# Eight tiles of the adaLN modulation move from the first phase to the fourth gate and the output projection

## The chip, the cores and the metric

The kernel runs on one core of a Trainium2 chip. The metric is device time in microseconds (us), the median of the runs shown; lower is better. Below, PE is the matrix engine (TensorE), DVE the vector engine, ACT the scalar engine, POOL GpSimd, and SP the engine that issues most DMAs.

## What is computed

One layer of a diffusion backbone over 256 latent tokens and 256 context tokens of width 2048, in float32:

```python
mod = silu(c) @ w_ada + b_ada                 # 6 x 2048 values: sh1, sc1, g1, sh2, sc2, g2
h  = rmsnorm(x) * (1 + sc1) + sh1             # hc likewise for the context
parts = split(h @ w_in)                       # ten projections of width 512
y  = sum_i sigmoid(h @ w_gate[i] + b_gate[i]) * (branch_i @ w_branch[i])   # 4 branches
x  = x + g1 * (y @ w_out)
h2 = rmsnorm(x) * (1 + sc2) + sh2
x  = x + g2 * ((silu(h2 @ w1) * (h2 @ w3)) @ w2)
```

The four branches are neighbourhood attention, a bidirectional gated DeltaNet, a Fourier mix and a spatial gating unit.

## The kernel before

Every weight streams through SBUF once. A weight tile is 1 MB (128 x 4 x 512 floats; in the first phase half of that). Each 1 MB tile is cut in two halves, and each half is split in two parts for accuracy: ACT casts it to `whi` (line 393), DVE subtracts to get `wlo` (line 395). PE then multiplies a half with 12 matmuls of 512 columns (hi x hi, lo x hi, hi x lo, for 2 k-tiles and 2 token tiles; lines 423 and 443), so a 1 MB tile is worth 24 matmuls.

The modulation needs 96 tiles of `w_ada`, 1 MB each, numbered t = 0 to 95. Two of them go over PE. Tiles below 32 (sh1, sc1) are multiplied twice on DVE, for latent and context (lines 358, 364). Each of the tiles 32 to 95 is one DVE instruction over 128 x 2048 floats with a sum (line 370), and a short read of the accumulator. These are the "later modulation": 32 to 47 are g1, 48 to 79 are sh2 and sc2 (needed when the second norm starts, `a2_lane`, line 1571), 80 to 95 are g2 (needed at the end).

The stages in order of time, with PE as the engine that all feed: the first phase (four projections of latent and context, in eight groups of two k-tiles, with the modulation tiles 0 to 31), the projections 7, 5, 6, 4, the gates 3, 2 and 0 with their branches (projection 8 inside gate 3), projection 9, the fourth gate (`gate_branch(1, ...)`, the DeltaNet's), the output projection, then w1/w3 and w2 of the feed-forward.

A list `plan` (lines 245 to 285) holds every load in one order, and SP issues the loads in it. `w_ada` tiles and all weight tiles after the first phase share one pool of three 1 MB buffers, `raw` (line 177; the half-size weight tiles of the first phase have two buffers of their own). A load is issued when a buffer is released: by the DVE multiplication for a `w_ada` tile, by the second `wlo` for a weight tile. `whi` and `wlo` have three buffers each (lines 178, 179), so a split runs at most two halves ahead of the half that PE reads. `queue` (line 248) spreads `n_ada` modulation tiles evenly behind the weight tiles of a stage:

```python
def queue(srcs, n_ada=0):
    for j, src in enumerate(srcs):
        plan.append(("w", src, 4))
        for _ in range(n_ada * (j + 1) // len(srcs) - n_ada * j // len(srcs)):
            if ada_rest:
                plan.append(("ada", ada_rest.pop(0), 4))
```

The first `ATAIL` of the later tiles stand in the first phase instead, two behind each of the four weight tiles of its last group (lines 246, 255, 262 to 267).

The order of instructions on each engine is fixed when the program is built. A small planner (`Issue`, line 61) keeps a model of the engines' clocks and takes steps of "lanes" (generators) as they come ready; `ada_lane` (line 330) gives a later tile to DVE when at least two halves stand ready for PE or when it has waited `slack` (0.5 us) after its modelled arrival (lines 366 to 371). On the chip each engine then works strictly through its own list.

Of the kernel before, what the change touches and what calls it, by code (L numbers as in the profile page):

```python
# [36 lines left out]
NMATS = 512  # L37

AHEAD = 3000
CFG = {'cvpos': 3, 'cv': 0, 'qv': 0, 'dn': 0, 'ev': 2000, 'evp': 0, 'evx': 0, 'evf': 0, 'evA': 0, 'ahead': 3000, 'adahp': 0, 'proj': {7: 2, 4: 2, 5: 2, 6: 2, 8: 2, 9: 2}, 'gate': {2: 1, 3: 1, 0: 1, 1: 3}, 'wout': [4, 4, 4, 0], 'hopp': 0.2, 'hopb': 0.25, 'hop': 0.2, 'win': 0.5, 'eps': 0.1, 'nz': 1, 'ndn': 11, 'nout': 4, 'groups': [[0, 2], [2, 2], [4, 2], [6, 2], [8, 2], [10, 2], [12, 2], [14, 2]], 'pe': [1, 18], 'pa': 5, 'atail': 8, 'nproj': 2, 'ngate': [9, 0, 8], 'start': 'a0 s0 x0 x1 s1 a16 w0 a1 a17 x2 w1 x3 w2 w3 s2 s3 s4', 'px1': 2, 'psp': 3, 'hoppA': 0.25, 'winA': 0.5, 'winA0': 1, 'hopA': 0.1, 'cw': [0, 0], 'ph1': 1, 'pseed': 0, 'pevac': 1, 'slack': 0.5}  # L40

GROUPS = tuple(tuple(g) for g in CFG.get('groups', ((0, 2), (2, 2), (4, 4), (8, 4), (12, 4))))


ATAIL = CFG['atail']
PE_ADA = tuple(CFG.get('pe',(0, 1, 2, 4, 5, 6, 7, 8, 10, 12, 14)))

# [6 lines left out]
class Event:  # L54


    def __init__(self):
        self.t = None


class Issue:
# [8 lines left out]
    def __init__(self):  # L70
        self.tune(CFG.get("hopA", CFG["hop"]), CFG.get("winA", CFG["win"]), CFG.get("hoppA", CFG["hopp"]), CFG.get("winA0", 3.0))
        self.now = 0.0
# [21 lines left out]
    def _turn(self, lane):  # L94
# [18 lines left out]
        else:  # L113
            window = self.win0 if lane[0] < 4 else self.win
            ready = lane[3] + ((self.HOP if lane[0] < 4 else CFG["hopb"]) if lane[5] not in (None, what) else 0.0)
            if ready > self.now + CFG["eps"] or self.clk[what] > self.now + window:
                return False
# [1731 lines left out]
```

## Time and profile before

| | us |
|---|---|
| median of 3 runs | 1753.32 (1749.28 to 1759.31) |
| the profiled execution's own time | 1752.79 |
| its span, first to last instruction | 1751.0 |
| PE busy / DVE busy / ACT busy in the span | 1702.5 / 1213.6 / 950.5 |
| later-modulation multiplications on DVE | 64, in 152.0 |
| mean granted TensorE clock | 0.998 |

Times in the rows are us from the start of the span. The ends of matmuls are modelled, so PE counts as busy through gaps shorter than a matmul; the count of matmuls in a stretch is the surer measure.

### The profile page before, as it was taken

The page shows a single profiled execution, that of the slowest core. Times are in us where ns is not written, and L with a number is a line of the kernel's source. Part 1 is how long each engine was busy: PE and PEld are TensorE (multiplying, and loading weights), DVE is VectorE, ACT ScalarE, POOL GpSimd, SP SyncE. Part 2 cuts the span into 40 slices and gives each one's busy share as a digit, 9 for nine tenths or more (in the row PEclk, how much of TensorE's full clock was granted, in tenths as well). Part 3 has the DMA queues.
Part 4 walks back from the last instruction along what each step waited for, and adds up shares of the span by engine and source line. Part 5 has one row for each costly group of instructions (what it writes and reads, how often), then busy time and mean ns, then how long its engine had stood idle before and what let it go on. Part 6 is the DMA issues. An engine that isn't in the chain of part 4 may idle for free.

```text
span 1751.0 us, 21765 instructions
## 1 busy us (share of the span) xinstructions
PE 1702.5 (97%) x8297; PEld 1395.0 (80%) x8297; DVE 1213.6 (69%) x1522; ACT 950.5 (54%) x1329; POOL 140.3 (8%) x136
## 2 busy tenths in 40 slices
PE   3999999999999999999999999999999999999998
PEld 2777887778788877988888878888888888888887
DVE  5999988885989865767776665555665555454554
ACT  5799977765556566235544474444444444433332
POOL 1000000210211153211101000000000000000000
PEclk9999999999999999999999999999999999999999
DMA  8677787656875655468777645666666655555553
GB/s 317 244 255 254 263 323 261 233 214 233 274 279 176 235 191 199 174 230 303 289 285 267 262 146 215 240 240 240 234 233 235 259 192 192 193 198 199 204 204 108
DMA packets 62461, 406.94 MB, mean 232 GB/s; under 512 B 7730, under 2 KB 8546, under 8 KB 16786
## 3 DMA queue, kind: packets, MB, share of 16 engines
q1 hardware_dynamic: 56164, 386.43, 60.4%
q0 software_dynamic: 4464, 16.49, 3.1%
q10 hardware_dynamic: 1728, 2.62, 0.4%
q8 instruction: 65, 1.06, 0.2%
q14 instruction: 40, 0.33, 0.0%
HBM read 401.29 MB, written 4.23 MB: 232 GB/s over the span
## 4 chain that ended last, share of the span: by engine, by line
PE 62%; issue 2%; POOL 1%; DMA 1%; ACT 0%; DVE 0%; POOLq 0%; ACTq 0%; DVEq 0%
PE acc L423 57%; PE acc L443 2%; POOL l L1177 1%; DMA raw<-w_gate 1%; PE ps L1694 1%; PE ps L1269 0%; POOL mg L1386 0%; PE ps L1258 0%; PE ps L1308 0%; PE ps L1211 0%; PE ps L1218 0%; PE ps L1280 0%; PE ps L1286 0%; PE ps L1290 0%; PE ps L1550 0%
## 5 line engine op out<-in xcount | busy, mean ns | idle before, releaser
L395 DVE TENSOR_TENSOR wlo<-raw,whi 128x1024 fp32r<-128x1024 f32 x532 | 667.9, 1257 | 422.0 <-ACT whi L393 416.9
L393 ACT CAST whi<-raw 128x1024 fp32r<-128x1024 f32 x532 | 560.3, 1055 | 574.1 <-PE acc L423 509.7
L423 PE MATMUL acc<-whi,hL 128*128 128x512 f32 x704 | 230.5, 398 | 0.0
L423 PE MATMUL acc<-whi,hH 128*128 128x512 f32 x704 | 224.5, 400 | 1.5 <-ACT acc L1361 0.8
L423 PE MATMUL acc<-wlo,hH 128*128 128x512 f32 x704 | 218.3, 391 | 1.0 <-DVE wlo L395 0.8
L423 PE MATMUL acc<-whi,h2L 128*128 128x512 f32 x684 | 213.4, 391 | 0.0
L423 PE MATMUL acc<-whi,h2H 128*128 128x512 f32 x684 | 211.8, 391 | 0.0
L423 PE MATMUL acc<-wlo,h2H 128*128 128x512 f32 x684 | 210.7, 389 | 0.0
L370 DVE SCALAR_TENSOR_TENSOR raw<-raw,cb 128x2048 f32<-128x2048 f32 x64 | 152.0, 2375 | 17.3 <-DMA raw<-w_ada 17.0
L423 PEld LDWEIGHTS acc<-wlo,hH 128*128 128x128 f32 x704 | 131.8, 188 | 30.4 <-DVE wlo L395 3.5
L423 PEld LDWEIGHTS acc<-whi,hL 128*128 128x128 f32 x704 | 132.3, 188 | 28.0 <-issue 0.7
L423 PEld LDWEIGHTS acc<-whi,hH 128*128 128x128 f32 x704 | 128.3, 189 | 28.5 <-ACT whi L393 1.4
L423 PEld LDWEIGHTS acc<-wlo,h2H 128*128 128x128 f32 x684 | 128.4, 188 | 26.7
L423 PEld LDWEIGHTS acc<-whi,h2L 128*128 128x128 f32 x684 | 128.4, 188 | 26.6
L423 PEld LDWEIGHTS acc<-whi,h2H 128*128 128x128 f32 x684 | 127.6, 188 | 26.1
L423 PE MATMUL acc<-whi,uL 128*128 128x512 f32 x340 | 105.0, 389 | 0.0
L423 PE MATMUL acc<-whi,uH 128*128 128x512 f32 x340 | 104.8, 389 | 0.0
L423 PE MATMUL acc<-wlo,uH 128*128 128x512 f32 x340 | 104.6, 389 | 0.0
L358 DVE SCALAR_TENSOR_TENSOR junk<-raw,cb 128x2048 bf16<-128x2048 f32 x30 | 68.6, 2285 | 11.3 <-ACT cb L522 11.2
L423 PEld LDWEIGHTS acc<-whi,uL 128*128 128x128 f32 x340 | 63.8, 188 | 13.3
L423 PEld LDWEIGHTS acc<-wlo,uH 128*128 128x128 f32 x340 | 63.8, 188 | 13.2
L423 PEld LDWEIGHTS acc<-whi,uH 128*128 128x128 f32 x340 | 63.7, 188 | 13.1
(390 smaller groups left out, 2161.9 us busy)
## 6 DMA issues: line engine op xcount, KB each, us to landing
raw<-w SPq DMA_DIRECT2D x132, 1024.0 KB, 4.8
raw<-w_ada SPq DMA_DIRECT2D x96, 1024.0 KB, 5.4
raw<-w_gate SPq DMA_DIRECT2D x64, 1024.0 KB, 4.9
raw<-w_in SPq DMA_DIRECT2D x24, 1024.0 KB, 5.6
raw<-w_in SPq DMA_DIRECT2D x32, 512.0 KB, 5.3
raw<-w_branch SPq DMA_DIRECT2D x16, 1024.0 KB, 4.9
raw<-w_out SPq DMA_DIRECT2D x16, 1024.0 KB, 4.8
bg<-b_gate POOLq DMA_DIRECT2D x16, 256.0 KB, 4.0
```

The lines of the kernel that those rows point to most:

```text
L358: V.scalar_tensor_tensor(junk, raw, 1.0, cb, ALU.mult, ALU.mult, accum_out=modA[:, 0, t:t + 1])
L370: V.scalar_tensor_tensor(raw, raw, 1.0, cb, ALU.mult, ALU.mult, accum_out=mod[:, t:t + 1])
L393: S.copy(hi, raws[e][:, 2 * q:2 * q + 2])
L395: V.tensor_tensor(lo, raws[e][:, 2 * q:2 * q + 2], hi.bitcast(F32), ALU.subtract)
L423: PE.matmul(acc, xx[:, kt0 + j, off:off + P], ww[:, j], start=start and n == 0 and not seeded, stop=stop and n == 5, skip_group_check=seeded)
L443: PE.matmul(acc[:, cs], xx[:, kt0 + j, off:off + P], ww[:, j, cs], start=n0 + n + i == 0, stop=n0 + n == 7 and i == 5, skip_group_check=c > 0)
L1177: G.tensor_tensor(dst.rearrange("p h (b i) -> p h b i", b=4), src[:, u0:u0 + 4].unsqueeze(2).to_broadcast([P, 4, 4, 32]), mats[:, M_BD:M_B ...
L1694: PE.transpose(tp[:, P * h:P * h + P], us[tt][:, P * h:P * h + P], ident)
```

## The change

`ATAIL` (`atail`) goes from 8 to 0, the fourth gate's share of modulation tiles (`ndn`) from 11 to 15 and the output projection's (`nout`) from 4 to 8. All other settings and all code are the same.

```diff
-CFG = {... 'ndn': 11, 'nout': 4, ... 'atail': 8, 'nproj': 2, 'ngate': [9, 0, 8], ...}
+CFG = {... 'ndn': 15, 'nout': 8, ... 'atail': 0, 'nproj': 2, 'ngate': [9, 0, 8], ...}
```

The tiles are taken from one list in order, so the numbers move up: the eight behind the projections are now 32 to 39 (they were 40 to 47), gate 3 has 40 to 48, gate 0 has 49 to 56, projection 9 has 57, the fourth gate 58 to 72 (was 66 to 76), the output projection 73 to 80 (was 77 to 80), and the feed-forward 81 to 95 as before. The count of tiles changes in three stages only: eight fewer in the first phase, four more in the fourth gate, four more in the output projection.

## Rows read from the trace of the kernel before

**Rows 1.** The page: busy us, share and instructions of each engine.
```profile
PE 1702.5 (97%) x8297; PEld 1395.0 (80%) x8297; DVE 1213.6 (69%) x1522; ACT 950.5 (54%) x1329; POOL 140.3 (8%) x136
```
**Rows 2.** Windows by stage: PE, PEld, DVE, ACT, POOL busy (count), clock, DMA share, GB/s.
```profile
40.00:205.00 165.00, 160.65 (x763) 128.55 (x762) 161.59 (x202) 151.38 (x298) 0.00 (x0) 1.00 0.71 251
205.00:239.30 34.30, 34.30 (x159) 28.05 (x158) 30.28 (x33) 30.42 (x58) 0.00 (x0) 1.00 0.90 333
239.30:330.00 90.70, 86.51 (x405) 69.77 (x404) 77.29 (x109) 67.44 (x93) 9.44 (x13) 0.98 0.71 258
804.80:916.00 111.20, 111.20 (x507) 92.00 (x507) 84.51 (x77) 56.72 (x65) 11.70 (x8) 1.00 0.77 285
916.00:982.70 66.70, 66.70 (x300) 55.22 (x299) 49.38 (x51) 31.48 (x38) 4.53 (x2) 1.00 0.74 272
```
**Rows 3.** Windows of line 370 alone: DVE busy (instructions, accumulator reads included).
```profile
205.00:239.30 34.30, 18.37 (x16) 1.00 0.90 333
804.80:916.00 111.20, 24.06 (x20) 1.00 0.77 285
916.00:982.70 66.70, 11.48 (x10) 1.00 0.74 272
```
**Rows 4.** The chain that ended last, a piece of the feed-forward: start us, us, what.
```profile
1199.22 41.53 PE acc L423 x183
```
**Rows 5.** What PE waited for between 236 and 330: total, times, longest.
```profile
PE ps L933 <- DVE rc L928: 2.5, 1, 2.5
PE ps L888 <- DVE kna L884: 1.6, 1, 1.6
```
**Rows 6.** Timeline of ACT, then DVE, 260 to 264: start, us, instruction [idle before].
```profile
260.25 1.05 ACT L393 CAST whi<-raw 128x1024 fp32r<-128x1024 f32 x1 [2.94 <-DMA raw<-w_in]
262.61 0.31 ACT L750 ACTIVATE rn<-sqs,gpar 128x16 f32<-128x16 f32 x1
...
263.24 0.69 DVE L884 TENSOR_TENSOR kna<-kna,rn 128x512 f32<-128x512 f32 x1
```
**Rows 7.** Timeline of SP's issues in the fourth gate, 849 to 883.
```profile
849.79 0.33 SPq L324 DMA_DIRECT2D raw<-w_ada  x1
855.12 0.33 SPq L324 DMA_DIRECT2D raw<-w_gate  x1
860.04 0.33 SPq L324 DMA_DIRECT2D raw<-w_ada  x1
861.18 0.33 SPq L324 DMA_DIRECT2D raw<-w_gate  x1
867.25 0.33 SPq L324 DMA_DIRECT2D raw<-w_gate  x1
868.39 0.33 SPq L324 DMA_DIRECT2D raw<-w_ada  x1
873.68 0.33 SPq L324 DMA_DIRECT2D raw<-w_gate  x1
882.81 0.33 SPq L324 DMA_DIRECT2D raw<-w_gate  x1
```
**Rows 8.** Timeline of DVE, 834 to 879: splits and multiplications that release those buffers.
```profile
834.44 2.29 DVE L370 SCALAR_TENSOR_TENSOR raw<-raw,cb 128x2048 f32<-128x2048 f32 x1 [2.08 <-DMA raw<-w_ada]
853.86 1.23 DVE L395 TENSOR_TENSOR wlo<-raw,whi 128x1024 fp32r<-128x1024 f32 x1 [1.49 <-ACT whi L393]
859.93 0.08 DVE L370 DVE_READ_ACCUMULATOR raw<-raw,cb 128x1 f32 x1
867.14 0.08 DVE L370 DVE_READ_ACCUMULATOR raw<-raw,cb 128x1 f32 x1
869.83 3.82 DVE L395 TENSOR_TENSOR wlo<-raw,whi 128x1024 fp32r<-128x1024 f32 x2 [0.28 <-ACT whi L393]
877.52 0.08 DVE L370 DVE_READ_ACCUMULATOR raw<-raw,cb 128x1 f32 x1
877.52 1.22 DVE L395 TENSOR_TENSOR wlo<-raw,whi 128x1024 fp32r<-128x1024 f32 x1
```
**Rows 9.** Timeline of PE: the first matmuls on two of those halves.
```profile
858.47 0.62 PE L423 MATMUL acc<-whi,hH 128*128 128x512 f32 x2
872.07 0.62 PE L423 MATMUL acc<-whi,hH 128*128 128x512 f32 x2
```
**Rows 10.** Windows around the wait for `rc`: columns as in Rows 2.
```profile
309.00:312.50 3.50, 1.03 (x9) 0.76 (x7) 3.43 (x8) 0.59 (x1) 1.23 (x1) 1.00 0.76 269
312.50:316.50 4.00, 4.00 (x19) 3.59 (x18) 2.38 (x5) 2.02 (x3) 0.00 (x0) 0.57 0.67 236
316.50:320.00 3.50, 3.50 (x23) 3.05 (x22) 1.90 (x5) 1.65 (x4) 0.00 (x0) 1.00 0.37 154
```

More of the change, by code (lines that the diff above doesn't have):

```diff
@@ L39 @@
 AHEAD = 3000
-CFG = {'cvpos': 3, 'cv': 0, 'qv': 0, 'dn': 0, 'ev': 2000, 'evp': 0, 'evx': 0, 'evf': 0, 'evA': 0, 'ahead': 3000, 'adahp': 0, 'proj': {7: 2, 4: 2, 5: 2, 6: 2, 8: 2, 9: 2}, 'gate': {2: 1, 3: 1, 0: 1, 1: 3}, 'wout': [4, 4, 4, 0], 'hopp': 0.2, 'hopb': 0.25, 'hop': 0.2, 'win': 0.5, 'eps': 0.1, 'nz': 1, 'ndn': 11, 'nout': 4, 'groups': [[0, 2], [2, 2], [4, 2], [6, 2], [8, 2], [10, 2], [12, 2], [14, 2]], 'pe': [1, 18], 'pa': 5, 'atail': 8, 'nproj': 2, 'ngate': [9, 0, 8], 'start': 'a0 s0 x0 x1 s1 a16 w0 a1 a17 x2 w1 x3 w2 w3 s2 s3 s4', 'px1': 2, 'psp': 3, 'hoppA': 0.25, 'winA': 0.5, 'winA0': 1, 'hopA': 0.1, 'cw': [0, 0], 'ph1': 1, 'pseed': 0, 'pevac': 1, 'slack': 0.5}
+CFG = {'cvpos': 3, 'cv': 0, 'qv': 0, 'dn': 0, 'ev': 2000, 'evp': 0, 'evx': 0, 'evf': 0, 'evA': 0, 'ahead': 3000, 'adahp': 0, 'proj': {7: 2, 4: 2, 5: 2, 6: 2, 8: 2, 9: 2}, 'gate': {2: 1, 3: 1, 0: 1, 1: 3}, 'wout': [4, 4, 4, 0], 'hopp': 0.2, 'hopb': 0.25, 'hop': 0.2, 'win': 0.5, 'eps': 0.1, 'nz': 1, 'ndn': 15, 'nout': 8, 'groups': [[0, 2], [2, 2], [4, 2], [6, 2], [8, 2], [10, 2], [12, 2], [14, 2]], 'pe': [1, 18], 'pa': 5, 'atail': 0, 'nproj': 2, 'ngate': [9, 0, 8], 'start': 'a0 s0 x0 x1 s1 a16 w0 a1 a17 x2 w1 x3 w2 w3 s2 s3 s4', 'px1': 2, 'psp': 3, 'hoppA': 0.25, 'winA': 0.5, 'winA0': 1, 'hopA': 0.1, 'cw': [0, 0], 'ph1': 1, 'pseed': 0, 'pevac': 1, 'slack': 0.5}
 GROUPS = tuple(tuple(g) for g in CFG.get('groups', ((0, 2), (2, 2), (4, 4), (8, 4), (12, 4))))
```

## The prediction

> **What bounds the kernel now.** I read the page first, then the windows by stage, then who waited for whom, and last the timelines of SP, DVE and PE in the stages whose load the change alters. The page says PE: 97% busy, DVE 69%, ACT 54% [rows 1]. Since PE's busy time hides short gaps, I checked it against a clean price. In the feed-forward 183 matmuls of 512 columns take 41.53 us, 0.227 each [rows 4], so a 1 MB weight tile (24 matmuls) is worth 5.45 us of PE. The fourth gate has 20 such tiles, 109 us by that price, and takes 111.2 us, its transposes included; the output projection's first twelve take 65 of 66.7 [rows 2]. PE has no idle time in either. In the end of the first phase (205 to 239.3), where the eight tiles are multiplied now, PE is also fed throughout: 34.3 busy of 34.3 us [rows 2]. The part of the first phase where DVE is the tight engine (161.6 of 165 us busy, PE 160.7) lies before it, from 40 to 205. None of the eight tiles is there: the window from 205 to 239.3 holds 16 instructions of line 370, eight multiplications and eight accumulator reads [rows 3].
>
> So the change takes work from a stretch in which PE does not wait and puts it into two in which PE does not wait. What it can bring or cost is second-hand: how early the weights of the next projection arrive, and whether the loads of the two later stages still keep up.
>
> **Removed from the first phase.** DVE loses 18.4 us of 30.3 busy in that window [rows 2, 3], and SP eight loads of 1.05 MB, 8.4 of the 11.4 MB that 333 GB/s moved in 34.3 us. On PE this is worth nothing there, since the splits already kept it fed. It is worth something just behind. SP issues loads in one order, so the weights of projection 7 now queue behind the last of the eight tiles. At 260.25 ACT still stands 2.94 us idle for a `w_in` tile; the `rn` activation, the `kna` product on DVE and PE's transposes of `kna` are queued behind that cast [rows 6], and PE waits 1.6 us for them [rows 5]. Without the eight loads ahead of them these weights arrive up to the length of eight loads earlier, with three buffers to hold them, so the 2.94 us go, and I take the 1.6 us of PE as gained. Bounds: nothing, if the planner places the normalisation later in its new order; and 1.6 + 2.5 us plus a clock loss if the wait for `rc` at 309 [rows 5] goes too. That wait is for a softmax chain of DVE and ACT which does not hang on a load, so I leave it. What comes late next after `kna` is this `rc`, unmoved.
>
> **Moved, at no cost.** The tiles behind the projections, gate 3, gate 0 and projection 9 change their numbers, not their count. g1 (32 to 47) is complete in gate 3 and read after gate 0; tile 79, the last that the second norm needs, is now the seventh of eight in the output projection. It comes two weight tiles (10.9 us) later than it did, with the last four weight tiles (22 us of PE) still to go before the norm starts. The feed-forward keeps its 15 tiles.
>
> **Added to the fourth gate and the output projection.** Four multiplications each. On DVE one is 2.4 us (24.06 / 10 and 11.48 / 5 [rows 3]); four are 9.5 us, and DVE goes from 84.5 to 94 of 111.2 us and from 49.4 to 59 of 66.7 [rows 2]. It has room. Bandwidth has room too: 35 tiles of 1.05 MB in 111.2 us are 330 GB/s and 20 in 66.7 are 314, where the end of the first phase moves 333 [rows 2]. The narrow place is the three buffers. SP issues a load only when one is released, and a weight load queued on SP behind a modulation load waits for that one's buffer as well. How long does a load hold a buffer, from issue to the last DVE instruction that reads it? For the modulation tiles issued at 849.79, 860.04 and 868.39 the accumulator reads end at 860.01, 867.22 and 877.60: 10.2, 7.2 and 9.2, mean 8.9 us. For the weight tiles issued at 861.18, 867.25 and 873.68 the second `wlo` ends at 873.65 and 878.74, and the third is done by 882.81, where the next issue falls: 12.5, 11.5 and 9.1, mean 11.0 [rows 7, 8].
>
> Three buffers carry 20 weight and 15 modulation tiles in (20 x 11.0 + 15 x 8.9) / 3 = 117.8 us. PE needs 111.2, so the loads fall 6.6 us behind. PE's lead absorbs some of it: a split that ends at 855.09 is first used at 858.47, 3.4 us later [rows 8, 9], counted half by half. That leaves 3.2 us. In the output projection, (12 x 11.0 + 8 x 8.9) / 3 = 67.7 against 66.7, 1.0 more, with no lead left to spend. The last four weight tiles have no modulation tile behind them and restore the lead. Sum: 4.2 us.
>
> The bounds are the ends of the same rows. With 9.1 and 7.2 the loads need 96.7 and 55.6 us: nothing is lost. With 12.5 and 10.2 they need 134.3 and 77.2, a loss of 23.1 - 3.4 + 10.5 = 30 us; but some of the long holds are a buffer waiting for PE to free a half, which costs nothing. The rows speak for the middle in one more way. The only place of the fourth gate where weight and modulation loads alternate twice (849.79 to 861.18), as three in four will after the change, is followed by the lead shrinking from 3.4 us to 0.6: two splits fill 869.83 to 873.65, and the first of them, done at about 871.5 (an estimate: near the middle), is used from 872.07 [rows 7 to 9]. The same list order can also hold DVE: at 834.44 it had stood 2.08 us for a late `w_ada` tile with the next splits queued behind it [rows 8].
>
> **The sum.** Own time of the profiled execution 1752.8 (span 1751.0 and 1.8 around it) - 1.6 + 4.2 = 1755.4. The median of the runs is 0.5 above that execution, so 1756.
>
> **A price that could come on top.** After the 2.5 us wait at 309 the granted clock is 0.57 over the next 4 us, near its lower level of 1.2 GHz for most of them, and 1.00 again behind [rows 10]: 0.43 x 4 = 1.7 us lost beside the wait. The wait of 1.6 us at 262 left no such mark; the mean of 0.98 over 90.7 us is that one fall [rows 2].
>
> The Trainium skill, "TensorE: Matmul & The Clock Gate", section "HAM oscillation", says that waits for loads between bursts of matmuls make the array fall back to half rate and start again cold. The row at 312.5 agrees for the longer wait, and the one at 262 shows a shorter one free of it. By that rule a loss of 4.2 us in two pieces would cost 3.4 more, and the time would be 1759; by the rows, pieces below 1.6 us cost only themselves, and the sum stays.
>
> **The rivals.**
> *The buffers carry it, and the front gains more.* The loads in the two stages take no more than PE does (holds of 10.4 and 8.5 or less), and the new order also avoids the wait for `rc` and its fall of the clock: 1752.8 - 1.6 - 2.5 - 1.7 = 1747.0, some 1747.5 on the median's scale. For it: 333 GB/s were sustained, and two of six holds are that short. Against: `rc` does not depend on loads.
> *The buffers bind, and it is slower.* With holds of 12.0 and 9.5 us, within what the rows show, the fourth gate's loads need 127.5 us and the output projection's 73.3: 12.9 + 6.6 = 19.5 us of PE waits, shown as casts that wait for `w_gate`, and the time is 1752.8 + 0.5 - 1.6 + 19.5 = 1771. It decides from holds of about 11.4 and 9.1, where the loss passes 10.4 us and the net 8.8. For it: the lead falls to 0.6 already with 11 tiles. Against: it recovers there within 15 us, and part of the holds is PE's own pace.
> *The list is planned anew and worse.* The planner's clock shifts from 213 us on, and every DVE list behind it is dealt afresh. Two more waits like that for `rc`, 2.5 + 1.7 each, on top of the forecast give 1764.
>
> **How the numbers follow.** The forecast, 1750 to 1762 with 1756 as its middle, 0.54. Buffers bind, 0.18; planned worse, 0.08; buffers carry and the front gains, 0.20. About 0.5% (8.8 us) is what a measurement of this kernel can tell from no change. Slower by more than that (above 1762.1): the binding rival whole and half of the badly planned one, 0.22. Faster by more (below 1744.5): a quarter of the gaining rival, 0.05. The rest, 0.73, is within. The range that leaves out two in ten runs from 1748, the gaining rival's middle, to 1769, inside the binding one.
>
> **What would show it.** After: eight multiplications gone from 205 to 239; no idle ACT before the first `w_in` casts, and no PE wait for `kna`; 15 and 8 multiplications in the two stages; ACT's waits there for `w_gate` and `w_out` longer, and PE waits of a few us in all for `whi` or `wlo` in lines 423 and 443, absent now. Matmul counts per us in the fourth gate falling from 507 in 111.2 would size the loss. The prediction is wrong if PE waits there exceed some 10 us or are nil, or if the time before 760 moves by more than 4 us.

## The result and the profile after

| | median us | runs | ratio to the kernel before |
|---|---|---|---|
| before | 1756.75 | 1749.28 to 1759.31 | |
| after | 1776.94 | 1774.16 to 1779.39 | 1.013 (95% interval 1.0114 to 1.0146) |

The change makes the kernel slower by some 20 us, 1.2 to 1.3%, beyond the forecast's range. (The medians alone give a ratio of 1.0115; 1.013 is the recorded ratio of all the runs, and both lie in its interval.) The profiled executions are 1751.0 and 1774.1 us long, 23.1 apart. To find where, I took the time of the first matmul of each stage: after the first phase a half of a weight tile is 12 matmuls of lines 423 and 443, so the first of a stage is found by counting. The steps between those times, after less before:

| stretch | before | after | step |
|---|---|---|---|
| start to the last group of the first phase | 0 to 215.5 | 0 to 216.4 | +0.9 |
| last group of the first phase | 215.5 to 238.9 | 216.4 to 248.4 | +8.7 |
| projections, gates 3, 2, 0, projection 9 | 238.9 to 810.3 | 248.4 to 822.1 | +2.2 |
| fourth gate | 810.3 to 923.0 | 822.1 to 942.2 | +7.4 |
| output projection, first three quarters | 923.0 to 989.2 | 942.2 to 1012.3 | +3.8 |
| from there to the end | 989.2 to 1751.0 | 1012.3 to 1774.1 | 0.0 |

The windows over those stretches, first of the kernel before (columns as in [rows 2]):

```profile
215.50:238.90 23.40, 23.40 (x110) 19.08 (x108) 19.38 (x22) 19.68 (x38) 0.00 (x0) 1.00 0.96 357
810.30:923.00 112.70, 112.70 (x514) 93.26 (x513) 86.54 (x80) 57.37 (x66) 11.94 (x9) 1.00 0.77 285
923.00:989.20 66.20, 66.20 (x298) 54.80 (x297) 47.23 (x48) 30.65 (x37) 4.30 (x2) 1.00 0.73 269
```

and of the kernel after:

```profile
216.40:248.40 32.00, 26.22 (x109) 21.11 (x108) 7.99 (x9) 22.19 (x40) 0.00 (x0) 0.89 0.24 77
822.10:942.20 120.10, 115.76 (x513) 92.34 (x512) 92.59 (x85) 55.25 (x66) 12.50 (x8) 1.00 0.80 300
942.20:1012.30 70.10, 68.58 (x298) 54.27 (x298) 57.57 (x58) 30.46 (x37) 3.52 (x2) 1.00 0.83 316
```

The matmul counts agree to one or two, so each stretch does the same PE work in more time. In the first of them, the end of the first phase ("the front" below), DVE is nearly idle (8 of 32 us), DMA at 0.24 of its share: nothing is short, and yet PE stands. The timeline of PE there says for what (start, us, instruction, idle before):

```profile
217.08 0.39 PE L697 MATMUL acc<-whi,hH 128*128 128x512 f32 x1
223.25 0.80 PE L697 MATMUL acc<-whi,hL 128*128 128x512 f32 x1 [5.78 <-DVE hL L617]
```

It needs `hL`, the low part of the last normalised tokens. DVE's timeline shows why `hL` is late:

```profile
213.11 1.21 DVE L395 TENSOR_TENSOR wlo<-raw,whi 128x1024 fp32r<-128x1024 f32 x1
214.25 0.28 DVE L589 TENSOR_SCALAR a<-modA,bp,cols 128x2 f32<-128x2 f32 x1
220.55 2.29 DVE L370 SCALAR_TENSOR_TENSOR raw<-raw,cb 128x2048 f32<-128x2048 f32 x1 [6.03 <-DMA raw<-w_ada]
222.77 0.08 DVE L370 DVE_READ_ACCUMULATOR raw<-raw,cb 128x1 f32 x1
222.77 0.42 DVE L617 TENSOR_TENSOR hL<-ps,hH 128x256 fp32r<-128x256 f32 x1
```

DVE works through a fixed list. In that list the product of tile 32, the first of the later modulation, stands ahead of `hL`; its load has not landed, DVE stands 6.03 us, and `hL` waits behind it. In the kernel before, the product of tile 32 had the same place, just ahead of `hL`, and did not wait:

```profile
213.52 2.28 DVE L370 SCALAR_TENSOR_TENSOR raw<-raw,cb 128x2048 f32<-128x2048 f32 x1
215.73 0.08 DVE L370 DVE_READ_ACCUMULATOR raw<-raw,cb 128x1 f32 x1
215.73 0.42 DVE L617 TENSOR_TENSOR hL<-ps,hH 128x256 fp32r<-128x256 f32 x1
```

So it is the load that moved. SP's timeline tells why it is late: projection 7's first two weight tiles now come ahead of it (two of the four loads in the first row, at 201.11 and 207.19) and fill two of the three buffers. It is issued only at 213.22, just behind the product that ends at 213.19 and releases the third.

```profile
201.11 10.23 SPq L324 DMA_DIRECT2D raw<-w_in  x4
213.22 0.33 SPq L324 DMA_DIRECT2D raw<-w_ada  x1
```

Before, tiles 32 and 33 were issued there, 13 us earlier for tile 32:

```profile
200.20 0.33 SPq L324 DMA_DIRECT2D raw<-w_ada  x1
206.28 0.33 SPq L324 DMA_DIRECT2D raw<-w_ada  x1
```

In the late stages the waits are shorter and many. Who waited for whom, in the fourth gate (total us, times, longest): ACT's casts, PE's loads of weights into the array (PEld), then PE's matmuls:

```profile
ACT whi L393 <- DMA raw<-w_gate: 37.2, 11, 5.5
ACT whi L393 <- DMA raw<-w_branch: 12.8, 4, 5.6
...
PEld acc L423 <- DVE wlo L395: 7.7, 9, 1.9
...
PE acc L423 <- DVE wlo L395: 3.9, 5, 1.5
```

The 7.7 us of PEld are close to the stage's loss of 7.4; PE itself shows less, since it counts as busy through short gaps. Before, the casts there waited some 12 us for loads, and the same view shows no wait of PE or PEld for a `wlo`:

```profile
ACT whi L393 <- DMA raw<-w_gate: 8.4, 3, 3.8
...
ACT whi L393 <- DMA raw<-w_branch: 3.3, 1, 3.3
```

So two new losses are there: one in the front, where I had booked a gain, and one in the late stages, 11.3 us where I had booked 4.2.

### The profile page after: what moved, and what is told of

Its sections match the earlier page's. It is cut to its first block, busy times and chain, and to the rows that moved or that the text cites. A ratio compares the mean times of both kernels' runs of the same rounds, so it can differ in the third digit from the quotient of the medians.

```text
span 1774.1 us, 21767 instructions
## 1 busy us (share of the span) xinstructions
PE 1712.5 (97%) x8297; PEld 1397.0 (79%) x8297; DVE 1211.9 (68%) x1522; ACT 947.0 (53%) x1328; POOL 143.2 (8%) x136
## 4 chain that ended last, share of the span: by engine, by line
PE 70%; DVE 5%; DMA 5%; issue 4%; POOL 1%; ACT 1%; DVEq 0%; ACTq 0%; POOLq 0%
PE acc L423 62%; DMA raw<-w_ada 3%; DVE wlo L395 2%; PE acc L443 2%; PE acc L697 1%; POOL l L1177 1%; DVE raw L370 1%; DMA raw<-w_gate 1%; PE ps L1694 1%; ACT whi L393 0%; DMA Lt<-scr 0%; DMA raw<-w_out 0%; PE ps L1269 0%; POOL mg L1386 0%; PE ps L940 0%
## 5 line engine op out<-in xcount | busy, mean ns | idle before, releaser
L423 PEld LDWEIGHTS acc<-whi,uL 128*128 128x128 f32 x340 | 63.8, 188 | 13.3
```

The lines of the kernel that those rows point to most:

```text
L423: PE.matmul(acc, xx[:, kt0 + j, off:off + P], ww[:, j], start=start and n == 0 and not seeded, stop=stop and n == 5, skip_group_check=seeded)
```

## The experiments

Each ratio is against runs of the kernel before on the same chip. The steps come from the profiled executions in the manner of the table above; steps over the start (0.3 to 3.4 us, differing between kernels with the same start) are left out. A step is read from one execution of each kernel, which can lie some us from the median of its runs.

**Front: is it the place in DVE's list?** (e1_order)

```diff
 # ada_lane, later tiles
+            if t == 32:
+                for s_ in range(2):
+                    for u in range(2):
+                        yield "wait", h_done[s_][KT - 1][u]
```

> The changed kernel with one product later in DVE's list: tile 32's multiplication is given to DVE only after the last h of the first phase; its load stays where it is. Theory F1 (the first later tile stands ahead of hL in DVE's list while its load still waits for a buffer): the 5.9 us wait and the slow clock behind it at 217 to 229 go, the first phase ends within 2 us of the kernel before (238.6) and not at 248.2, and the time is 1766 to 1769. Rival F2 (the loads of projection 7, now further ahead, delay the last group, and the order matters little): the wait moves to another instruction, the first phase still ends after 245, and the time stays at 1774 to 1779. Both: the fourth gate and the output projection still lose 10 to 12 us against the kernel before.

Measured 1769.9 us, ratio 1.0105 (1.0088 to 1.0122). The wait is gone. The window of the last group:

```profile
215.80:239.10 23.30, 23.30 (x109) 19.21 (x108) 7.76 (x9) 20.92 (x40) 0.00 (x0) 1.00 0.27 98
```

23.3 us for the same matmuls, as before the change, at a full clock. DVE's list there now reads:

```profile
215.38 0.42 DVE L621 TENSOR_TENSOR hL<-ps,hH 128x256 fp32r<-128x256 f32 x1 [1.46 <-ACT hH L619]
217.61 0.42 DVE L621 TENSOR_TENSOR hcL<-ps,hcH 128x256 fp32r<-128x256 f32 x1 [1.81 <-ACT hcH L619]
218.58 2.29 DVE L374 SCALAR_TENSOR_TENSOR raw<-raw,cb 128x2048 f32<-128x2048 f32 x1 [0.55 <-DMA raw<-w_ada]
```

F1 holds, F2 falls: the loads were not moved. The time is 0.9 us above F1's range. The stretch from the projections to projection 9 is 4.1 us longer than before (+2.2 in the changed kernel), and the late stages lose 5.3 + 3.4, less than the 10 to 12 expected. The profiled execution, the fastest of four (1765.8), is 10.0 us shorter than the changed kernel's; by the ratios the whole gain is smaller.

**Back alone.** (e2_back)

```diff
-'ndn': 11, 'nout': 4, ... 'atail': 8, 'nproj': 2
+'ndn': 15, 'nout': 8, ... 'atail': 8, 'nproj': 0
```

> The kernel before with its eight tiles left in the first phase (atail 8), the eight behind the projections taken away (nproj 0) and ndn 15, nout 8: the second half of the change alone. Theory B (the loss of the fourth gate and the output projection belongs to the 15 and 8 tiles there, whatever comes first): the steps of these stages are 7 and 4 us longer than before, the first phase ends as before, and the time is 1763 to 1768 (up to 4 us of waits in the projections may go). Rival: these stages lose only because the front left the planner's clock and the chip's apart; then the steps are as before and the time is 1752 to 1757.

Measured 1764.61 us, ratio 1.0074 (1.0059 to 1.0089). The front keeps its time; the fourth gate loses 10.0 us and the output projection 5.2, against the 7 and 4 expected. The loss belongs to the 15 and 8 tiles, with either front, and its size differs with the order that the planner deals. Part of the 10.0 us is the clock: DVE stands 4.75 us for one load, PE 4.42 us behind it, and the granted clock is then 0.50 for 6.8 us.

```profile
869.21 2.29 DVE L370 SCALAR_TENSOR_TENSOR raw<-raw,cb 128x2048 f32<-128x2048 f32 x1 [4.75 <-DMA raw<-w_ada]
873.30 1.22 PE L423 MATMUL acc<-wlo,hH 128*128 128x512 f32 x2 [4.42 <-DVE wlo L395]
```

```profile
872.70:879.50 6.80, 6.20 (x15) 4.74 (x16) 6.80 (x5) 0.97 (x2) 3.91 (x2) 0.50 0.88 319
```

Half of PE's 6.20 us there, 3.1, is what the clock cost (an estimate); that leaves 6.9, near the 7 expected. Between the projections and projection 9 this kernel gains 5.5 us. The projections, from which modulation tiles were taken, give only 0.6 of it, and gates 3, 2 and 0 the rest (-5.0, +3.9, -3.8).

**Buffers, bandwidth or order in the late stages?** (e4_buf4, e5_short, e6_delay, e8_buf4_delay, each on the changed kernel)

```diff
 # e4_buf4: dma_lane; the pool and the ring follow `own`
+                own = kind == "ada" and 58 <= src <= 80 and src % 2 == 0
+                depth = 2 if kind == "w8" else 1 if own else 3     # own: tile of dp, tag "kTd"
 # e5_short: ada_lane
+            n_ = 8 if 58 <= t <= 80 and t % 2 == 0 else D
+            V.scalar_tensor_tensor(raw[:, 0:n_], raw[:, 0:n_], 1.0, cb[:, 0:n_], ...)
 # e6_delay: ada_lane, behind the wait for arrived[e]
+            if 58 <= t <= 80:
+                yield "delay", 2.5
```

> The changed kernel with a fourth 1 MB buffer in the fourth gate and the output projection: the tiles of even number from 58 to 80 load into the DeltaNet's kTd tile, which nothing reads by then. Loads and products are all there. Theory B1 (three buffers held too long): the two stages lose 2 us or less of their 11.3, time 1766 to 1769. Rival B2 (the DMA engines carry no more): they lose the same, 1774 to 1779. Rival B3 (a product that waits for its load holds the splits behind it on DVE): about half goes, 1770 to 1773.

> The changed kernel with the multiplications of the twelve tiles of even number from 58 to 80 cut to 8 of 2048 columns, so part of the modulation is left out; their loads are all there. A hold of such a tile falls from 8.6 to about 6.3 us. Theory B1 (buffers): (20 x 11.9 + 7 x 8.6 + 8 x 6.3) / 3 = 116.2 us of loads in the fourth gate, where PE needs 112.7: the stage loses 3 to 4 us and not 7.4, the output projection nothing, time 1768 to 1771. Rival B2 (bandwidth): 1774 to 1779, the same steps as the changed kernel. Rival B3 (DVE held by a late load): the waits stay, since a short product waits for its load as a long one does; 1774 to 1777.

> The changed kernel with the products of tiles 58 to 80 given to DVE 2.5 us later by the planner, three buffers as before. If the splits held behind a product whose load is late (theory B3) make most of the 11.3 us of the two late stages, these stages lose 5 us or less and the time is 1769 to 1772. If the holds of three buffers do (B1), a later product holds its buffer no shorter, and the stages lose as much as in the changed kernel or more: 1775 to 1783.

> The changed kernel with the fourth buffer and the later products together. With the buffer alone the two late stages still lost 3.1 us, 2.7 of it where a product waited 2.67 us for its load with splits queued behind it. Theory (buffers first, DVE's order for the rest): the stages lose 1 us or less, time 1763 to 1766. Rival (the rest is bandwidth): 3 us stay, 1766 to 1769.

| kernel | median us | ratio (95%) | fourth gate | output projection | DVE idle for `w_ada` loads there |
|---|---|---|---|---|---|
| before | | | 0 | 0 | 6.1 |
| after | 1776.94 | 1.013 (1.0114 to 1.0146) | +7.4 | +3.8 | 11.6 |
| fourth buffer | 1767.17 | 1.0087 (1.0072 to 1.0102) | +3.1 | 0.0 | 13.3 |
| short products | 1768.35 | 1.0093 (1.0078 to 1.0108) | +3.7 | +1.1 | 8.7 |
| later products | 1768.24 | 1.0086 (1.0067 to 1.0105) | +3.9 | +0.6 | 1.7 |
| buffer and later products | 1764.73 | 1.0063 (1.0046 to 1.008) | 0.0 | 0.0 | 1.7 |

The fourth buffer met B1's time and nearly its loss (3.1 where 2 was set); short products did too (3.7 and 1.1 where 3 to 4 and nothing were set), though they also take work from DVE (77.8 us busy in the fourth gate against 92.6). But later products did what B3 foretold, with three buffers: 4.5 us are left of 11.3, and 0.7 more come at the very end of the output projection, as with short products. The modulation tiles were held no shorter: from issue to the last DVE instruction that reads the tile, the mean over both stages is 9.2 us, against 8.4 in the changed kernel. The weight tiles' holds fell, from 12.0 to 10.9. So B1 alone is not the cause. What the fourth buffer leaves is one place, in DVE's timeline:

```profile
881.31 0.68 DVE L1383 TENSOR_TENSOR gs<-gs,acc 128x512 f32<-128x512 f32 x1
884.65 2.29 DVE L372 SCALAR_TENSOR_TENSOR raw<-raw,cb 128x2048 f32<-128x2048 f32 x1 [2.67 <-DMA raw<-w_ada]
886.87 0.08 DVE L372 DVE_READ_ACCUMULATOR raw<-raw,cb 128x1 f32 x1
886.87 2.35 DVE L397 TENSOR_TENSOR wlo<-raw,whi 128x1024 fp32r<-128x1024 f32 x2
```

A product stands for its load, and two splits start the moment it is done: the front's picture again. With both cures the windows of the two stages are:

```profile
822.90:935.50 112.60, 112.60 (x513) 93.20 (x512) 94.03 (x88) 57.30 (x67) 13.94 (x9) 1.00 0.84 325
935.50:1001.80 66.30, 66.30 (x298) 54.87 (x297) 54.87 (x54) 30.42 (x37) 3.22 (x2) 1.00 0.81 317
```

All 15 and 8 tiles are loaded and multiplied, at 325 and 317 GB/s, in the time of the kernel before. That rules out B2. The two causes work on each other: a load waits for a buffer and lands late, DVE stands at its product, and the splits behind it keep their own buffers longer. The weight tiles' shorter holds with later products agree with that. Relief at either end takes off 52 to 73% of the loss (8.2 of 11.3 with the buffer; 5.8 with short products and 6.1 with later ones, with the 0.7 at the end counted), both take all of it.

**All three cures at once.** (e10_all: e1, the buffer, the later products)

> The changed kernel with tile 32's product behind the last h of the first phase, the fourth buffer and the later products. If the three causes found so far are all that matters, what is left of the 20 to 24 us is the steps between the projections and projection 9, 2 to 5 us: 1754 to 1758. If the causes give way to one another (a wait removed comes back in the next stage), 1760 or more.

Measured 1757.41 us, ratio 1.0022 (1.0011 to 1.0034), within the first expectation: front 0.0, late stages 0.0, and 5.2 us between the projections and projection 9.

**One cure for front and back?** (e12_delay_all: the changed kernel, `yield "delay"` of 1.5 us for tiles 32 to 57 and 2.5 for 58 to 80, three buffers)

> The changed kernel with every later product given to DVE later: 1.5 us for tiles 32 to 57, 2.5 us for 58 to 80; three buffers, all loads as changed. If one cause (the planner gives DVE a product before its load has landed, and the work queued behind waits) makes the front's wait and most of the late stages' loss, the wait at 217 shrinks to 2 us or less, the first phase ends within 3 us of the kernel before, the late stages lose 4 to 6 us, and the time is 1758 to 1763. If the front needs another cure (1.5 us is less than the 6 us that DVE stood), it stays at 1766 to 1769.

Measured 1763.65 us, ratio 1.0062 (1.004 to 1.0084), just above the first expectation. The front's loss falls from 8.7 to 2.4; there DVE still stands 3.2 us for tile 32 with `hcL` behind it. The late stages lose 5.3 + 0.4, a PE wait of 2.4 us and 3.4 us at half clock behind it among them. So one cause is at work in both places, DVE standing at a product whose load is late; the delay was too short for the front, and in the late stages the buffers add to it.

**A better version.** (e9_best: e2 with the buffer and the later products; e11_best: and 1.5 us for the tiles below 58; e13_before_delay: the kernel before with e12's delays alone)

> The eight tiles back in the first phase, none behind the projections, 15 and 8 in the two late stages, with the fourth buffer and the later products. The same distribution with three buffers reached projection 9's end 5.5 us earlier than its own first phase would give and then lost 15.1. If buffers and order are the whole of that loss, it is 1747 to 1751, faster than the kernel before by 1 to 5 us; if some 3 us of it is bandwidth, 1750 to 1754.

Measured 1753.97 us, ratio 0.9995 (0.9982 to 1.0008): the first expectation missed. The time lies in the second, but not for its reason, bandwidth: the late stages lost 1.1 and 0, and a product in gate 3 stood for its load, with PE behind it (DVE's row, then PE's):

```profile
486.72 2.29 DVE L374 SCALAR_TENSOR_TENSOR raw<-raw,cb 128x2048 f32<-128x2048 f32 x1 [2.32 <-DMA raw<-w_ada]
486.86 0.61 PE L427 MATMUL acc<-whi,hL 128*128 128x512 f32 x2
490.21 1.22 PE L427 MATMUL acc<-wlo,hH 128*128 128x512 f32 x2 [2.74 <-DVE wlo L399]
```

> The kernel of the run before with eight tiles in the first phase, none behind the projections, 15 and 8 late, and a fourth buffer, now with the products of tiles 40 to 57 given to DVE 1.5 us later too. In that run a product at 486.7 stood 2.3 us for its load, PE waited 2.9 us for the split behind it, and the clock fell for 6.8 us. If that is the same cause as in the late stages, both go: 1747 to 1751, faster than the kernel before. If the new order moves the wait elsewhere in gate 3: 1752 to 1756.

Measured 1743.59 us, ratio 0.9947 (0.9929 to 0.9965): faster than the kernel before by 0.5%, and by more than I expected. The gain lies between the projections and projection 9 (-11.5 us; the fourth gate lost 1.6). The projections give 0.6 of it, gate 3 9.0 and gate 0 4.0, and gate 2 takes 2.1 back. PE's windows from 330 to 560, of the kernel before and of this one:

```profile
330.00:560.00 230.00, 227.48 (x1082) 186.61 (x1081) 195.10 (x396) 137.26 (x191) 34.79 (x51) 1.00 0.68 240
```

```profile
330.00:560.00 230.00, 230.00 (x1094) 191.44 (x1093) 194.56 (x391) 138.63 (x187) 31.71 (x49) 1.00 0.68 243
```

PE has no gap left there, at the same DMA share and the same load on DVE. That window holds 2.5 us of the gain. From 239 on to the fourth gate PE's waits are 3.3 us where they were 10.0, and no time is at half clock where 3.4 us were; together this is worth 8.4, and the rest of the 11.5 is in no gap that the profile shows.

> The kernel before, its distribution of tiles unchanged, with the same later products (1.5 us for tiles 32 to 57, 2.5 us above). PE waits for no such product there, so if the delay only cures that wait, the time is that of the kernel before within 4 us: 1750 to 1757. If later products cost by themselves (buffers held longer, no lead to pay for it), 1757 or more.

Measured 1746.73 us, ratio 0.9966 (0.9952 to 0.9979), faster than expected. I had thought that only waits of PE for a product's split count. From the projections to projection 9 this kernel gains 7.1 us. PE's waits there fall from 10.0 us to 5.2, with the one for `rc` [rows 5] gone and 0.2 left of the one for `kna`, and DVE's for `w_ada` loads from 8.1 to 4.5. That the products' waits on DVE had delayed the branches is the likely reading, not a shown one: the delay also has the planner deal every list behind it anew. Of the best version's 0.5%, 0.3% goes with this cure alone; the rest goes with the new distribution and the fourth buffer (the two intervals overlap a little, and no run parts them).

## Why the prediction was wrong

**The front: the step that failed.** "Removed from the first phase ... on PE this is worth nothing there" and the gain of 1.6 behind it. I counted what eight instructions less are worth to DVE and to the queue, and took the rest of DVE's list as given. But the product of tile 32 kept its place just ahead of `hL`, where PE waits on DVE's next instruction, while its load went behind projection 7's weights in SP's queue, from 200.20 to 213.22. The lead of that load was the term put at nothing. That is +8.7 us: 5.8 of wait and the rest a slow clock. The prediction's own sign of being wrong, the time before 760 moving by more than 4 us, came true: it moved by some 12. I had seen the pattern [rows 8] (DVE standing 2.08 us for a late `w_ada`, with splits behind) and named it for the late stages only, without a price. What is queued behind a product's wait had to be asked of tile 32 too.

**What went as said there.** PE's wait for `kna` is gone, and so are ACT's waits for `w_in` between 240 and 300 (10.4 us before); in the projections (248 to 332) PE waits 3.5 us in one piece, for the softmax chain, where it had waited 2.5 and 1.6 [rows 5]. So the chain, which the prediction left unmoved, took 1.0 of the 1.6 us back: the stretch from projection 7 to gate 3 gained 0.6. That the earlier loads ended the wait for `kna` is not shown: it is gone in e2 too, where the eight tiles stay.

**The late stages: the mechanism was right, the size was not.** The three buffers fell behind as worked out, casts waited for `w_gate`, and the lead was spent. The terms of 3.2 and 1.0 measured 7.4 and 3.8. The loss is a small difference between two large sums: three buffers over 120.1 us and 35 tiles are 10.3 us a load where I had priced 10.1. The mis-sized term is the weight tiles' hold: 12.0 us in the mean over both stages where 11.0 was priced (the modulation tiles' was 8.4, for 8.9), and (20 x 12.0 + 15 x 8.4) / 3 is 122 us, not 117.8. What made it longer, and what the sum left out, is DVE's order: with later products alone more than half of the 11.3 us go. The windows that the prediction took for the two stages also begin 5.5 and 7 us early (804.8 and 916 for 810.3 and 923.0); by the true 112.7 and 66.2 us its terms would have been 1.7 and 1.5, a little further off. The rival "the buffers bind" priced this at 19.5, too much; its total, 1771, is the nearest of all the cases to the 1777 by luck, since it knew nothing of the front.

**The rival "planned anew and worse"** had 0.08. What it foretold, other lists behind 213 us and a longer wait for the softmax chain, is in the 2.2 us between the projections and projection 9. The front's loss is another: there the product kept its place, and the load came late.

**The price that could come on top** was paid in the front only; the fall behind the softmax chain's wait was there before and stayed. After PE's 5.8 us wait the granted clock is 0.50 for 6.8 us (1.2 GHz), at 222 to 228.8, and none of the late stages' waits, 1.5 us the longest, brought it down:

```profile
222.00:228.80 6.80, 5.55 (x13) 4.45 (x14) 2.65 (x5) 2.35 (x4) 0.00 (x0) 0.50 0.47 154
```

So in this kernel the rows were the better guide for the late stages than the 3.4 us of the other reckoning. But "pieces below 1.6 us cost only themselves" does not hold in every run: see the last section.

**Still open.** The 2.2 us between the projections and projection 9 in the changed kernel (4.1 and 5.2 in e1 and e10). Where they are can be read: in PE's waits and in the time at half clock, of which I count half as lost (an estimate). From the first projection to the fourth gate, in us:

| kernel | PE's waits | time at half clock | waits and half of that, over before | step |
|---|---|---|---|---|
| before | 10.0 | 3.4 | | |
| after | 12.4 | 3.4 | +2.4 | +2.2 |
| e1_order | 11.3 | 10.2 | +4.7 | +4.1 |
| e10_all | 12.4 | 10.2 | +5.8 | +5.2 |
| e2_back | 6.3 | 0.0 | -5.4 | -5.5 |
| e13_before_delay | 5.2 | 3.4 | -4.8 | -7.1 |

In the changed kernel the longest are the softmax chain and the DeltaNet's `l`:

```profile
PE ps L933 <- DVE lg L929: 5.3, 2, 3.5
PE ps L1188 <- POOL l L1177: 3.8, 3, 1.9
```

Why these waits grow or shrink stays open: the planner deals these lists anew whenever something before them moves, and no run here takes one piece of that alone.

## What to carry to other kernels

Where lists are fixed at build time, a load moved is a wait moved: look up which instruction of which engine consumes it, what stands behind that instruction, and who waits for that, for the first tile of the new order as for the added ones. A stage whose buffers are priced within a few per cent of the time it has must be read as a loss of unknown size, not as the difference. And a product that nobody waits for can stand late in its engine's list: here that alone, without moving a tile, went with a gain of 0.3% (0.2 to 0.5).

## What was not expected of the hardware

Two stages of some 180 us in all ran at 325 and 317 GB/s of 1 MB loads with PE fed throughout (e8); the end of the first phase before the change had moved 357 at a DMA share of 0.96. After PE's wait of 2.74 us in e9 the granted clock was 0.50 for 6.8 us:

```profile
489.60:496.40 6.80, 6.19 (x16) 4.82 (x17) 6.56 (x21) 2.32 (x3) 1.73 (x1) 0.50 0.78 242
```

After the one of 2.5 us in the kernel before, it was 0.57 over 4 us [rows 10], and after 1.6 us it did not fall. The length of the wait does not settle it. In e4 a wait of 1.55 us was followed by 3.4 us at half clock, and in e6 one of 3.58 us by none (each wait, then the window behind it):

```profile
787.17 0.73 PE L425 MATMUL acc<-whi,hH 128*128 128x512 f32 x2 [1.55 <-ACT whi L395]
```

```profile
788.70:792.10 3.40, 3.40 (x9) 2.65 (x9) 3.19 (x3) 1.81 (x2) 0.00 (x0) 0.50 0.52 166
```

```profile
308.78 0.63 PE L935 MATMUL ps<-mats,lg 128*128 128x128 f32 x4 [3.58 <-DVE lg L931]
```

```profile
308.80:316.00 7.20, 7.20 (x43) 6.18 (x44) 5.50 (x11) 6.22 (x10) 2.31 (x2) 1.00 0.80 296
```
